# Larger row tiles for a fused residual add and RMS norm: two x slots of 7 rows and a shared residual area in place of three slots of 6 rows

## The chip, the cores and the metric

The kernel runs on one core of a Trainium2 chip. The metric is the device time of one execution in microseconds (us). Nine executions of the kernel before on one chip lie within 1.1 to 1.7 us of each other (the four of the first comparison within 0.7 us), so differences of 1 to 4 us, a tenth of a per cent of the time, can be told apart only with several runs on the same chip.

## The reference

```python
x, residual: float32 [32, 2048, 2048]; gamma: float32 [2048]; eps = 1e-6
z = x + residual
rms = np.sqrt(np.mean(z ** 2, axis=-1, keepdims=True) + eps)
return (z / rms * gamma).astype(np.float32)
```

There are 65,536 rows of 2048 floats (8 KiB each), 512 rows for each of the 128 partitions. Each element is read twice from memory (x and residual) and written once, 1610.6 MB in all.

## The kernel before

A tile has R rows in every partition. Partition p of a tile holds R consecutive rows, so one DMA moves 128 runs, one per partition, of R x 8 KiB. Three slots hold x, and then z and the result in place; one slot holds the residual.

```python
R = 6
NZ = 3
sizes = ([left] if left else []) + [R] * n_full      # 2 rows, then 85 tiles of 6
z_slots = [slots.tile([P, R, D], fp32, name=f"z{k}") for k in range(NZ)]
r_slot = slots.tile([P, R, D], fp32, name="r_slot")
gamma_tile = slots.tile([P, D], fp32, name="gamma_tile")

def compute(i):
    # ... the last tile: pieces of 2 rows, the scale one piece behind ...
    groups = [(a, min(a + 3, sizes[i])) for a in range(0, sizes[i], 3)]
    rms_of = []
    for a, b in groups:
        add(i, a, b)                     # VectorE: z = x + r
        rms_of.append(square(i, a, b))   # ScalarE: sum of squares of each row, then sqrt
    for (a, b), rms in zip(groups, rms_of):
        scale(i, a, b, rms)              # VectorE: 1/rms, then z * rstd * gamma, row by row

load_x(0); load_r(0); load_gamma(); load_x(1); load_r(1)
compute(0)
for i in range(1, n_tiles):
    store(i - 1)
    if i + 1 < n_tiles:
        load_x(i + 1)
    compute(i)
    if i + 1 < n_tiles:
        load_r(i + 1)
store(last)
```

All loads and stores of x, residual and output are issued by SyncE, on one queue; gamma is loaded by ScalarE's queue.

Of the kernel before, what the change touches and what calls it, by code (L numbers as in the profile page):

```python
# [1 line left out]

# [4 lines left out]


@with_exitstack
def kernel(  # L10
    ctx: ExitStack,
    tc: tile.TileContext,
    x: bass.AP,
    residual: bass.AP,
    gamma: bass.AP,
    eps: float,
    out: bass.AP,
):





    nc = tc.nc
    P = nc.NUM_PARTITIONS
    fp32 = mybir.dt.float32
    Act = mybir.ActivationFunctionType
    mult = mybir.AluOpType.mult

    x_f = x.flatten_outer_dims()  # L30
    r_f = residual.flatten_outer_dims()
    o_f = out.flatten_outer_dims()

    n_rows, D = x_f.shape
    R = 6
    NZ = 3
    n_full = n_rows // (P * R)
    left = (n_rows - n_full * P * R) // P
    assert n_full * P * R + left * P == n_rows
    sizes = ([left] if left else []) + [R] * n_full  # L40
    starts = [0]
    for k in sizes:
        starts.append(starts[-1] + P * k)
    n_tiles = len(sizes)
    assert n_tiles >= 4

    def rows(t, i):
        k = sizes[i]
        a = starts[i]
        return t[a : a + P * k, :].rearrange("(p r) m -> p r m", r=k)  # L50

    inv_d = 1.0 / float(D)

    slots = ctx.enter_context(tc.tile_pool(name="slots", bufs=1))
    stats = ctx.enter_context(tc.tile_pool(name="stats", bufs=6))
    psum = ctx.enter_context(tc.tile_pool(name="psum", bufs=1, space=bass.MemoryType.PSUM))

    z_slots = [slots.tile([P, R, D], fp32, name=f"z{k}") for k in range(NZ)]
    r_slot = slots.tile([P, R, D], fp32, name="r_slot")
    gamma_tile = slots.tile([P, D], fp32, name="gamma_tile")  # L60
    eps_tile = slots.tile([P, 1], fp32, name="eps_tile")
    sq_junk = psum.tile([P, D], fp32, name="sq_junk")
    nc.vector.memset(eps_tile, float(eps))  # L63

    last = n_tiles - 1
    piece = 2

    def pieces(i):
        k = sizes[i]
        return [(a, min(a + piece, k)) for a in range(0, k, piece)] if i == last else [(0, k)]  # L70

    def r_of(i):

        return z_slots[NZ - 1] if i == 0 else r_slot

    def load_x(i):
        nc.sync.dma_start(out=z_slots[i % NZ][:, : sizes[i], :], in_=rows(x_f, i))  # L77

    def load_r(i):
        for a, b in pieces(i):  # L80
            nc.sync.dma_start(out=r_of(i)[:, a:b, :], in_=rows(r_f, i)[:, a:b, :])  # L81

    def store(i):
        for a, b in pieces(i):
            nc.sync.dma_start(out=rows(o_f, i)[:, a:b, :], in_=z_slots[i % NZ][:, a:b, :])

    def add(i, a, b):
        z = z_slots[i % NZ]
        nc.vector.tensor_add(out=z[:, a:b, :], in0=z[:, a:b, :], in1=r_of(i)[:, a:b, :])  # L89

    def square(i, a, b):
        n = b - a
        ssq = stats.tile([P, 3], fp32, name="ssq")
        for g in range(n):
            nc.scalar.activation(  # L95
                out=sq_junk,
                in_=z_slots[i % NZ][:, a + g, :],
                func=Act.Square,
                accum_out=ssq[:, g : g + 1],
            )  # L100
        rms = stats.tile([P, 3], fp32, name="rms")
        nc.scalar.activation(  # L102
            out=rms[:, :n], in_=ssq[:, :n], func=Act.Sqrt, bias=eps_tile, scale=inv_d
        )
        return rms

    def scale(i, a, b, rms):
        n = b - a
        rstd = stats.tile([P, 3], fp32, name="rstd")
        nc.vector.reciprocal(out=rstd[:, :n], in_=rms[:, :n])  # L110
        for g in range(n):
            row = z_slots[i % NZ][:, a + g, :]
            nc.vector.scalar_tensor_tensor(  # L113
                out=row,
                in0=row,
                scalar=rstd[:, g : g + 1],
                in1=gamma_tile,
                op0=mult,
                op1=mult,
            )  # L120

    def compute(i):
        if i == last:
            before = None
            for a, b in pieces(i):
                add(i, a, b)
                rms = square(i, a, b)
                if before is not None:
                    scale(i, *before)
                before = (a, b, rms)  # L130
            scale(i, *before)
            return
        groups = [(a, min(a + 3, sizes[i])) for a in range(0, sizes[i], 3)]
        rms_of = []
        for a, b in groups:
            add(i, a, b)
            rms_of.append(square(i, a, b))
        for (a, b), rms in zip(groups, rms_of):
            scale(i, a, b, rms)


    def load_gamma():
        nc.vector.memset(gamma_tile, 0.0)  # L143
        for q in range(4):
            nc.scalar.dma_start(
                out=gamma_tile[32 * q : 32 * q + 1, :], in_=gamma.partition_broadcast(1)
            )
        nc.vector.stream_shuffle(gamma_tile, gamma_tile, [0] * 32)  # L148

    load_x(0)  # L150
    load_r(0)
    load_gamma()
    load_x(1)
    load_r(1)
    compute(0)
    for i in range(1, n_tiles):
        store(i - 1)
        if i + 1 < n_tiles:
            load_x(i + 1)
        compute(i)  # L160
        if i + 1 < n_tiles:
            load_r(i + 1)
    store(last)


# [1 line left out]
_INS = ['x', 'residual', 'gamma', 'eps']  # L167
_OUTS = [((32, 2048, 2048), 'float32')]

_NUMBERS = {'eps': 9.999999974752427e-07}  # L170


# [26 lines left out]
```

## Time and profile before

| | before |
|---|---|
| time, median of 4 runs | 3728.59 us (3728.27 to 3728.93) |
| bytes moved | 1610.6 MB, 432 GB/s over the span |
| DMA engines busy | 100.0% of the span |
| VectorE, ScalarE busy | 62%, 29% |

The lines below are from the page of the kernel before: the span, the busy time of the engines, the DMA rows of the table of 40 slices (busy tenths, then GB/s), and the queue table (packets, MB, share of the 16 DMA engines).

```profile
span 3726.4 us, 2716 instructions
DVE 2312.2 (62%) x860; ACT 1079.1 (29%) x1198; POOL 0.2 (0%) x4
...
DMA  9999999999999999999999999999999999999999
GB/s 421 431 434 433 433 435 431 434 434 433 433 434 432 436 432 432 436 431 434 434 432 434 434 433 435 432 433 436 431 434 434 433 436 433 433 435 432 435 434 398
...
q1 hardware_dynamic: 37728, 1610.63, 100.0%
q14 instruction: 20, 0.16, 0.0%
```

The DMA row has no slice below nine tenths. The queue q1, which carries all loads and stores, fills the 16 engines for the whole span. In this steady part nothing that makes VectorE or ScalarE faster can be expected to help; only fewer bytes, cheaper transfers, or less time in which the DMA stands still. Queue q14 is the fetching of instructions, 20 packets of 8 KiB.

What the DMA queue itself waits for before it can issue (the waits of SyncE's queue; columns: who, for what, us in total, times, longest) shows how far ahead it runs:

```profile
SPq L81 <- DMA r_slot<-in_residual_dram: 1294.7, 84, 16.5
SPq L85 <- DVE z L113: 1192.4, 87, 20.8
SPq L81 <- DVE rstd L110: 1107.2, 84, 13.3
```

L81 is the residual load, L85 the store. SyncE waits most of the time, but it does so with earlier transfers queued, so the waits cost nothing. This has to be checked for each change: a wait of the issuing queue is free only while something else is still in the queue.

One more view is needed, which the page only sums up: the packet records of the trace. Every packet has a start and a duration, and one DMA ends with 16 semaphore packets, one from each engine. From these the following can be read for each engine:

```
packet        most frequent duration (before)
8 KiB run     309 ns
16 KiB run    611 ns
48 KiB run    1815 ns   (24,834 of 32,384)
semaphore     9 ns
time from one semaphore packet to the next on one engine (8 packets of 48 KiB and a semaphore): 14,500 ns
```

The 16 engines do not finish together. In the profiled run of before the median engine's last semaphore packet comes 3718.9 us after the first packet, the slowest engine's at 3723.4 us. The records carry no engine number: "slowest" and "median" are read from the 16 semaphore packets of each DMA, sorted by time.

### The profile page before, as it was taken

How to read it: one execution, taken by the hardware profiler on the slowest of the kernel's cores; microseconds unless marked ns; L12 is line 12 of the kernel's file. 1: busy time of each engine (PE TensorE's matmuls, PEld its weight loads, DVE VectorE, ACT ScalarE, POOL GpSimd, SP SyncE). 2: the span in 40 equal slices, each digit the busy share in tenths (PEclk: the TensorE clock that was granted, in tenths of full speed). 3: DMA queues.
4: the chain of work that ended last, by engine and by line, in shares of the span. 5: the costliest groups of instructions: out<-in, count | busy, mean ns of one | idle time of the engine just before them, and what ended most of it. 6: DMA issues, size and time to landing. Idle time of an engine off the chain costs nothing.

```text
span 3726.4 us, 2716 instructions
## 1 busy us (share of the span) xinstructions
DVE 2312.2 (62%) x860; ACT 1079.1 (29%) x1198; POOL 0.2 (0%) x4
## 2 busy tenths in 40 slices
DVE  5665556666655666665566666556666655566666
ACT  2322222332222233222223332222233222223322
POOL 0000000000000000000000000000000000000000
DMA  9999999999999999999999999999999999999999
GB/s 421 431 434 433 433 435 431 434 434 433 433 434 432 436 432 432 436 431 434 434 432 434 434 433 435 432 433 436 431 434 434 433 436 433 433 435 432 435 434 398
DMA packets 37756, 1610.83 MB, mean 432 GB/s; under 512 B 4196, under 2 KB 4196, under 8 KB 4196
## 3 DMA queue, kind: packets, MB, share of 16 engines
q1 hardware_dynamic: 37728, 1610.63, 100.0%
q14 instruction: 20, 0.16, 0.0%
q10 hardware_dynamic: 8, 0.03, 0.0%
HBM read 1073.77 MB, written 536.87 MB: 432 GB/s over the span
## 4 chain that ended last, share of the span: by engine, by line
DMA 69%; DVE 30%; issue 0%; DVEq 0%; SPq 0%
DMA r_slot<-in_residual_dram 69%; DVE z L89 30%; DVE z L113 0%; DVE rstd L110 0%; DVEq L194 0%; DVEq L89 0%; SPq L77 0%; SPq L81 0%
## 5 line engine op out<-in xcount | busy, mean ns | idle before, releaser
L89 DVE TENSOR_TENSOR z<-z,r_slot 128x6144 f32<-128x6144 f32 (+1 forms) x171 | 1107.6, 6517 | 1380.4 <-DMA r_slot<-in_residual_dram 1380.4
L95 ACT ACTIVATE sq_junk<-z 128x2048 f32<-128x2048 f32 x512 | 963.5, 1882 | 2620.5 <-DVE z L89 2604.1
L113 DVE SCALAR_TENSOR_TENSOR z<-z,rstd,gamma_tile 128x2048 f32<-128x2048 f32 x512 | 1173.8, 2348 | 6.1
L95 ACT ACTIVATION_READ_ACCUMULATOR sq_junk<-z 128x1 f32 x512 | 95.5, 186 | 0.0
L102 ACT ACTIVATE rms<-ssq,eps_tile 128x3 f32<-128x3 f32 (+1 forms) x172 | 51.0, 296 | 5.5
L110 DVE RECIPROCAL rstd<-rms 128x3 f32<-128x3 f32 (+1 forms) x172 | 29.7, 172 | 3.3 <-ACT rms L102 3.2
L89 DVE TENSOR_TENSOR z<-z,z 128x4096 f32<-128x4096 f32 x1 | 4.4, 4426 | 11.4 <-DMA z<-in_residual_dram 11.4
L95 ACT ACT_TABLE_LOAD x1 | 1.3, 1283 | 4.4 <-issue 4.4
L148 DVE STREAM_SHUFFLE gamma_tile<-gamma_tile 128x2048 f32<-128x2048 f32 x1 | 2.5, 2536 | 0.0
L143 DVE MEMSET gamma_tile<- 128x2048 f32 x1 | 1.8, 1765 | 0.4 <-issue 0.4
L102 ACT ACT_TABLE_LOAD x1 | 1.3, 1283 | 0.0
L63 DVE MEMSET eps_tile<- 128x1 f32 x1 | 0.1, 59 | 0.8 <-PEq L180 0.8
L180 POOL MEMSET const-bfloat16-1.0<- 128x1 bf16 x1 | 0.1, 101 | 0.0
L180 POOL MEMSET const-uint8-127<- 128x1 uint8 x1 | 0.1, 101 | 0.0
L180 POOL MEMSET const-float32-0.0<- 128x1 f32 x1 | 0.1, 98 | 0.2 <-issue 0.2
L180 POOL MEMSET const-float32-1.0<- 128x1 f32 x1 | 0.1, 98 | 0.0
L148 DVE LOAD_MASK_SELECT gamma_tile<-gamma_tile x1 | 0.0, 14 | 0.0
## 6 DMA issues: line engine op xcount, KB each, us to landing
z<-in_x_dram SPq DMA_DIRECT2D x85, 6144.0 KB, 44.9
r_slot<-in_residual_dram SPq DMA_DIRECT2D x84, 6144.0 KB, 30.4
out_dram<-z SPq DMA_DIRECT2D x84, 6144.0 KB, 30.8
out_dram<-z SPq DMA_DIRECT2D x4, 2048.0 KB, 15.1
r_slot<-in_residual_dram SPq DMA_DIRECT2D x3, 2048.0 KB, 27.3
z<-in_x_dram SPq DMA_DIRECT2D x1, 2048.0 KB, 7.8
z<-in_residual_dram SPq DMA_DIRECT2D x1, 2048.0 KB, 13.2
gamma_tile<-in_gamma_dram ACTq DMA_DIRECT2D x4, 8.0 KB
```

Source lines behind the costliest of these rows:

```text
L63: nc.vector.memset(eps_tile, float(eps))
L89: nc.vector.tensor_add(out=z[:, a:b, :], in0=z[:, a:b, :], in1=r_of(i)[:, a:b, :])
L95: nc.scalar.activation(out=sq_junk, in_=z_slots[i % NZ][:, a + g, :], func=Act.Square, accum_out=ssq[:, g : g + 1],)
L102: nc.scalar.activation(out=rms[:, :n], in_=ssq[:, :n], func=Act.Sqrt, bias=eps_tile, scale=inv_d)
L110: nc.vector.reciprocal(out=rstd[:, :n], in_=rms[:, :n])
L113: nc.vector.scalar_tensor_tensor(out=row, in0=row, scalar=rstd[:, g : g + 1], in1=gamma_tile, op0=mult, op1=mult,)
L143: nc.vector.memset(gamma_tile, 0.0)
L148: nc.vector.stream_shuffle(gamma_tile, gamma_tile, [0] * 32)
L180: nc = _bacc.Bacc("TRN2", target_bir_lowering=False, num_devices=1)
```

## The change

The intent is to use the on-chip memory for longer runs: 56 KiB in place of 48, so fewer DMAs and fewer packets for the same bytes. Two x slots of 7 rows and a residual area of 11 rows take the place of three x slots and one residual slot of 6 rows. Residual tiles enter the area at row 0 or row 4 in turn, so the next residual tile overlaps the present one only in three rows, and those three rows are added first. Gamma moves to PSUM. 512 = 73 x 7 + 1, so the first tile has 1 row.

```diff
-    R = 6
-    NZ = 3
+    R = 7
+    STEP = 4
...
-    z_slots = [slots.tile([P, R, D], fp32, name=f"z{k}") for k in range(NZ)]
-    r_slot = slots.tile([P, R, D], fp32, name="r_slot")
-    gamma_tile = slots.tile([P, D], fp32, name="gamma_tile")
+    z_slots = [slots.tile([P, R, D], fp32, name=f"z{k}") for k in range(2)]
+    r_area = slots.tile([P, R + STEP, D], fp32, name="r_area")
+    gamma_tile = psum.tile([P, D], fp32, name="gamma_tile")
...
+    def entry(i):
+        if i == 0:
+            return R + STEP - left
+        return 0 if i % 2 else STEP
+
+    tail = [(0, 3), (3, 5), (5, 7)]
+
+    def parts(i):
+        if i == 0:
+            return [(0, left)]
+        return [(STEP, R), (0, STEP)] if i % 2 else [(0, R - STEP), (R - STEP, R)]
...
     load_x(0)
     load_r(0)
     load_gamma()
-    load_x(1)
     load_r(1)
     compute(0)
-    for i in range(1, n_tiles):
+    store(0)
+    load_x(1)
+    load_x(2)
+    compute(1)
+    load_r(2)
+    for i in range(2, n_tiles):
         store(i - 1)
-        if i + 1 < n_tiles:
-            load_x(i + 1)
         compute(i)
         if i + 1 < n_tiles:
             load_r(i + 1)
+            load_x(i + 1)
     store(last)
```

With two slots, x of tile i+1 goes where tile i-1 was, so its load must wait until store(i-1) has landed. Before, it waited for store(i-2), which had landed long ago.

More of the change, by code (lines that the diff above doesn't have):

```diff
@@ L34 @@
     n_rows, D = x_f.shape
-    R = 6
-    NZ = 3
+    R = 7
+    STEP = 4
     n_full = n_rows // (P * R)
     left = (n_rows - n_full * P * R) // P
-    assert n_full * P * R + left * P == n_rows
-    sizes = ([left] if left else []) + [R] * n_full
+    assert n_full * P * R + left * P == n_rows and 0 < left <= STEP
+    sizes = [left] + [R] * n_full
     starts = [0]
@@ L44 @@
     n_tiles = len(sizes)
-    assert n_tiles >= 4
+    last = n_tiles - 1
+    assert n_tiles >= 5
     def rows(t, i):
         k = sizes[i]
-        a = starts[i]
-        return t[a : a + P * k, :].rearrange("(p r) m -> p r m", r=k)
+        return t[starts[i] : starts[i] + P * k, :].rearrange("(p r) m -> p r m", r=k)
     inv_d = 1.0 / float(D)
@@ L63 @@
     nc.vector.memset(eps_tile, float(eps))
-    last = n_tiles - 1
-    piece = 2
-    def pieces(i):
-        k = sizes[i]
-        return [(a, min(a + piece, k)) for a in range(0, k, piece)] if i == last else [(0, k)]
-    def r_of(i):
-        return z_slots[NZ - 1] if i == 0 else r_slot
+    def entry(i):
[7 more added lines that the diff above has]
+        return [(STEP, R), (0, STEP)] if i % 2 else [(0, R - STEP), (R - STEP, R)]
@@ L76, in load_x, with load_r @@
+    def load_r(i):
+        a = entry(i)
+        nc.sync.dma_start(out=r_area[:, a : a + sizes[i], :], in_=rows(r_f, i))
     def load_x(i):
-        nc.sync.dma_start(out=z_slots[i % NZ][:, : sizes[i], :], in_=rows(x_f, i))
-    def load_r(i):
-        for a, b in pieces(i):
-            nc.sync.dma_start(out=r_of(i)[:, a:b, :], in_=rows(r_f, i)[:, a:b, :])
+        for a, b in tail if i == last else [(0, sizes[i])]:
+            nc.sync.dma_start(out=z_slots[i % 2][:, a:b, :], in_=rows(x_f, i)[:, a:b, :])
@@ L83, in store @@
     def store(i):
-        for a, b in pieces(i):
-            nc.sync.dma_start(out=rows(o_f, i)[:, a:b, :], in_=z_slots[i % NZ][:, a:b, :])
+        for a, b in tail if i == last else [(0, sizes[i])]:
+            nc.sync.dma_start(out=rows(o_f, i)[:, a:b, :], in_=z_slots[i % 2][:, a:b, :])
     def add(i, a, b):
-        z = z_slots[i % NZ]
-        nc.vector.tensor_add(out=z[:, a:b, :], in0=z[:, a:b, :], in1=r_of(i)[:, a:b, :])
+        z = z_slots[i % 2][:, a:b, :]
+        o = entry(i)
+        nc.vector.tensor_add(out=z, in0=z, in1=r_area[:, o + a : o + b, :])
@@ L91, in square @@
     def square(i, a, b):
         n = b - a
-        ssq = stats.tile([P, 3], fp32, name="ssq")
+        ssq = stats.tile([P, 4], fp32, name="ssq")
         for g in range(n):
@@ L96, in square @@
                 out=sq_junk,
-                in_=z_slots[i % NZ][:, a + g, :],
+                in_=z_slots[i % 2][:, a + g, :],
                 func=Act.Square,
@@ L100, in square @@
             )
-        rms = stats.tile([P, 3], fp32, name="rms")
+        rms = stats.tile([P, 4], fp32, name="rms")
         nc.scalar.activation(
@@ L108, in scale @@
         n = b - a
-        rstd = stats.tile([P, 3], fp32, name="rstd")
+        rstd = stats.tile([P, 4], fp32, name="rstd")
         nc.vector.reciprocal(out=rstd[:, :n], in_=rms[:, :n])
         for g in range(n):
-            row = z_slots[i % NZ][:, a + g, :]
+            row = z_slots[i % 2][:, a + g, :]
             nc.vector.scalar_tensor_tensor(
@@ L124, in compute @@
             before = None
-            for a, b in pieces(i):
+            for a, b in tail:
                 add(i, a, b)
@@ L132, in compute @@
             return
-        groups = [(a, min(a + 3, sizes[i])) for a in range(0, sizes[i], 3)]
-        rms_of = []
-        for a, b in groups:
+        done = []
+        for a, b in parts(i):
             add(i, a, b)
-            rms_of.append(square(i, a, b))
-        for (a, b), rms in zip(groups, rms_of):
-            scale(i, a, b, rms)
+            done.append((a, b, square(i, a, b)))
+        for d in done:
+            scale(i, *d)
     def load_gamma():
-        nc.vector.memset(gamma_tile, 0.0)
+        row = R + STEP - left - 1
+        stage = r_area[:, row, :]
+        nc.vector.memset(stage, 0.0)
         for q in range(4):
             nc.scalar.dma_start(
-                out=gamma_tile[32 * q : 32 * q + 1, :], in_=gamma.partition_broadcast(1)
+                out=r_area[32 * q : 32 * q + 1, row, :], in_=gamma.partition_broadcast(1)
             )
-        nc.vector.stream_shuffle(gamma_tile, gamma_tile, [0] * 32)
+        nc.vector.stream_shuffle(gamma_tile, stage, [0] * 32)
     load_x(0)
```

## The prediction

> **What bounds the kernel now.** The DMA engines. The profile's table of slices has them at nine tenths or more in all 40 slices, the queue table gives the one load/store queue 100.0% of the 16 engines' span, at 432 GB/s mean (433 to 434 in the middle). VectorE is busy 62%, ScalarE 29%. The Trainium skill, "DMA: Bandwidth & Descriptors", section Bandwidth, gives 435.2 GB/s as the ceiling of the 16 ports; this trace agrees at 434.
>
> **What a packet costs.** The packet records are sharply peaked: 8 KiB in 309 ns, 16 KiB in 611 ns, 48 KiB in 1815 ns (24,834 of 32,384 exactly so). That is a line: 27.2 bytes per ns plus about 9 ns per packet; a semaphore packet is 9 ns more. A 56 KiB packet is then 2116 ns (estimate from this line).
>
> **What the change removes.** Bytes stay at 1610.6 MB. Load/store DMAs fall from 262 to 226, so each engine runs 8 x 36 = 288 packets and 36 semaphore packets fewer: 324 x 9 ns = 2.9 us of about 3720 us per engine. That is on the critical path.
>
> **What it adds.** With two x slots, x(i+1) must wait for store(i-1) to land. In steady state this is hidden: a tile is three transfers of 8 x 2116 ns = 16.9 us, in order store(i-1), residual(i+1), x(i+1). The residual load waits only for tile i's first add (3 rows, 6.55 us), which ends some 10 us before store(i-1) does; x(i+1) can be issued some 15 us before the residual load ends; and a tile's compute (about 33.5 us: adds 15.3, then 7 scales of 2.35 behind squares of 1.88 + 0.19) fits well inside the 50.8 us period. I expect no starvation per tile.
>
> One gap at the start: after x(1) lands, only x(2) and residual(2), 33.9 us, are queued, while store(1) needs 33.5 us of compute, then issue and start (a load's packets begin about 1.6 us after issue, estimated by aligning packet and instruction records). Most engines go idle about 3 us once; those that lag (about 2 us behind by then in the semaphore packets) 1 to 2 us. The laggards set the end: before, most engines finish about 4.5 us ahead of the last. So this costs some 1.5 us. At the end the pieces (3, 2, 2 rows) are ready before the queue reaches them; neutral. Gamma in PSUM and larger adds touch only VectorE, off the path.
>
> **Sum.** 3728.7 - 2.9 + 1.5 = 3727.3 us. Range 3723 to 3732. Faster by over 2%: 1%; within 2%: 98%; slower by over 2%: 1%.
>
> **What would show the steps right or wrong.**
> - Packets 37,756 before, near 32,600 after; 56 KiB packets at 2116 ns.
> - DMA share full in every slice; mean 432 GB/s again.
> - DMA queue's waits: residual load released by the first add, x load by the store's landing, both while earlier transfers run. In the timeline store(1) is issued near 80 us, about when residual(2) ends, and DMA dips just after.
> - VectorE near 2305 us; the gamma-in-PSUM scale near 2.35 us.
>
> **What would make it wrong.** The residual load waiting for both adds or a later VectorE instruction; a start latency of stores of many us, so that the queue runs dry per tile (each us per tile is 73 us, 2%); the 56 KiB address pitch suiting memory worse or better than 48 KiB; lagging engines lagging further, which the mean share would hide.

## The result

| | before | changed |
|---|---|---|
| time, median of 4 runs | 3728.59 us (3728.27 to 3728.93) | 3730.61 us (3729.46 to 3732.38) |
| ratio | | 1.0006, 95% interval 0.9988 to 1.0023 |
| span of the profiled run | 3726.4 us | 3728.7 us |

A ratio is the mean time of one kernel's runs over that of the other's of the same rounds, so it is not quite the ratio of the medians. By the ratio alone the two are the same. Repeated twice more with 5 runs each, on chips 12 and 13, the changed kernel took 3731.40 (3730.44 to 3733.40) beside 3728.79 (3728.07 to 3729.14), and 3730.68 (3729.40 to 3731.89) beside 3728.79 (3728.05 to 3729.37). In each of the three comparisons its fastest run is above the slowest of before: it is about 2 us slower, where the prediction expected 1.4 us faster.

The page of the changed kernel, the same lines:

```profile
span 3728.7 us, 2557 instructions
DVE 2301.9 (62%) x812; ACT 1071.7 (29%) x1174; POOL 0.2 (0%) x4
...
DMA  9999999999999999999999999999999999999999
GB/s 408 423 433 433 434 433 434 433 434 435 433 433 433 433 433 434 434 434 434 434 433 435 434 434 433 433 433 433 433 434 434 434 435 434 434 434 434 433 433 403
...
q1 hardware_dynamic: 32544, 1610.63, 99.9%
q14 instruction: 20, 0.16, 0.0%
```

Packets are down as planned. The middle of the run is as fast as before or a little faster; the first two slices, 408 and 423 against 421 and 431, are slower. The waits of the DMA queue (L82 is the residual load, L90 the store, L86 the x load):

```profile
SPq L82 <- DVE z L95: 1682.0, 72, 24.6
SPq L90 <- DVE z L119: 1195.0, 75, 32.0
SPq L86 <- DMA out_dram<-z: 717.9, 72, 11.5
```

The third line is the new dependence: 72 times the x load waited for a store to land. It looks like the cost of the change at first sight. The periods say otherwise: from 300 to 3600 us a DMA of 7 rows takes the median engine 16,920 ns, or 2417.1 ns per row, against 14,512 ns, or 2418.7 ns per row, before. Over 512 x 3 = 1536 rows that is 2.4 us less. So the wait is hidden, as predicted. On the slowest engine the same stretch shows no saving, 2421.0 to 2422.0 ns per row in three profiled runs of the changed kernel against 2420.8 before; the records further below tell why.

The slow first slices are seen in the timeline of SyncE's queue (start us, us, engine, line, instruction, what it moves):

```profile
20.55 0.35 SPq L90 DMA_DIRECT2D out_dram<-z  x1
20.95 10.05 SPq L86 DMA_DIRECT2D z<-in_x_dram  x2
54.10 0.33 SPq L82 DMA_DIRECT2D r_area<-in_residual_dram  x1
80.54 0.34 SPq L90 DMA_DIRECT2D out_dram<-z  x1
88.03 0.33 SPq L82 DMA_DIRECT2D r_area<-in_residual_dram  x1
```

x(2) and residual(2) are the only work behind x(1). Store(1) is issued at 80.54 us, when residual(2) has already ended on nearly all engines. The same stretches by windows (from:to in us, length, busy time and count of VectorE, ScalarE and GpSimd, PE clock, DMA share, GB/s), first of before and then of the changed kernel:

```profile
70.00:78.00 8.00, 2.35 (x2) 0.00 (x0) 0.00 (x0) 1.00 0.99 430
78.00:82.00 4.00, 2.87 (x1) 0.00 (x0) 0.00 (x0) 1.00 1.08 467
82.00:90.00 8.00, 8.00 (x2) 4.22 (x5) 0.00 (x0) 1.00 0.96 418
```

```profile
70.00:78.00 8.00, 6.79 (x4) 1.11 (x3) 0.00 (x0) 1.00 0.96 416
78.00:82.00 4.00, 3.07 (x3) 0.00 (x0) 0.00 (x0) 1.00 0.57 244
82.00:90.00 8.00, 8.00 (x2) 1.97 (x2) 0.00 (x0) 1.00 0.98 423
```

From 78 to 82 us the DMA moves 244 GB/s in place of 467: the queue has run dry once. (Short windows hold few packets of 2 us each, so a share can come out above 1.) In the records the idle time there is 2.6 us, averaged over the engines.

There is a second dry stretch, which was not predicted, near 3706 us: 3.2 us of mean idle time. At the end of the run VectorE does all three adds of the last tile before the first scale, although the code writes a scale between the second and the third. The scheduler had reordered them.

```profile
3684.31 15.23 DVE L95 TENSOR_TENSOR z<-z,r_area 128x6144 f32<-128x6144 f32 x3 [8.18 <-DMA z<-in_x_dram]
...
3701.67 11.36 DVE L119 SCALAR_TENSOR_TENSOR z<-z,rstd,gamma_tile 128x2048 f32<-128x2048 f32 x5
```

The kernel before has an idle stretch in its tail as well, of 1.2 us. The windows of the tail, of before and then of the changed kernel (mind the different ends):

```profile
3700.00:3710.00 10.00, 9.93 (x7) 4.74 (x8) 0.00 (x0) 1.00 0.84 360
```

```profile
3702.00:3710.00 8.00, 8.00 (x4) 3.75 (x5) 0.00 (x0) 1.00 0.51 222
```

So 2.6 us of mean idle time at the start and 3.2 - 1.2 = 2.0 us more in the tail stand against 2.4 us saved. The simple sum, 2.6 + 2.0 - 2.4 = 2.2 us, is just what the profiled runs differ by. The experiments show that this sum is nevertheless the wrong explanation: it fits by chance.

### The profile page after: what moved, and what is told of

It reads as the page before. It is cut to its first block, busy times and chain, and to the rows that moved or that the text cites. A ratio compares the mean times of both kernels' runs of the same rounds, so it can differ in the third digit from the quotient of the medians.

```text
span 3728.7 us, 2557 instructions
## 1 busy us (share of the span) xinstructions
DVE 2301.9 (62%) x812; ACT 1071.7 (29%) x1174; POOL 0.2 (0%) x4
## 2 busy tenths in 40 slices
DMA packets 32572, 1610.82 MB, mean 432 GB/s; under 512 B 3620, under 2 KB 3620, under 8 KB 3620
## 4 chain that ended last, share of the span: by engine, by line
DMA 67%; DVE 24%; ACT 8%; issue 0%; DVEq 0%; ACTq 0%; SPq 0%
DMA z<-in_x_dram 33%; DMA out_dram<-z 33%; DVE z L95 15%; DVE z L119 9%; ACT sq_junk L101 8%; DMA r_area<-in_residual_dram 1%; DMA r_area<-in_gamma_dram 0%; ACT rms L108 0%; DVE rstd L116 0%; DVE gamma_tile L155 0%; DVEq L204 0%; DVE r_area L150 0%; ACTq L152 0%; DVEq L95 0%; SPq L90 0%
## 5 line engine op out<-in xcount | busy, mean ns | idle before, releaser
L95 DVE TENSOR_TENSOR z<-z,r_area 128x6144 f32<-128x6144 f32 (+3 forms) x148 | 1109.0, 7535 | 1293.7 <-DMA z<-in_x_dram 1287.1
L116 DVE RECIPROCAL rstd<-rms 128x3 f32<-128x3 f32 (+3 forms) x148 | 25.6, 173 | 111.1 <-ACT rms L108 111.1
L108 ACT ACTIVATE rms<-ssq,eps_tile 128x3 f32<-128x3 f32 (+3 forms) x148 | 43.9, 297 | 4.8
## 6 DMA issues: line engine op xcount, KB each, us to landing
r_area<-in_residual_dram SPq DMA_DIRECT2D x73, 7168.0 KB, 27.2
```

What stands on the lines that cost most here:

```text
L95: nc.vector.tensor_add(out=z, in0=z, in1=r_area[:, o + a : o + b, :])
L108: nc.scalar.activation(out=rms[:, :n], in_=ssq[:, :n], func=Act.Sqrt, bias=eps_tile, scale=inv_d)
L116: nc.vector.reciprocal(out=rstd[:, :n], in_=rms[:, :n])
```

## The experiments

The theories:

- **A.** The slowest of the 16 DMA engines sets the end. The loss is the dry stretch near 80 us, as far as that engine feels it, and slow packets after it; the dry stretch in the tail costs nothing, because the slowest engine is behind and never runs dry there.
- **B.** Every microsecond of mean idle time counts, at the start and in the tail.
- **C.** The loss is in the steady state: two slots or the 56 KiB runs.

Eleven kernels ran, one of them (the changed kernel unaltered) twice, so twelve runs. All gave correct results.

| run | time, median us (range) | before on the same chip |
|---|---|---|
| after_again (changed kernel) | 3731.40 (3730.44 to 3733.40) | 3728.79 |
| start_fix | 3732.22 (3731.09 to 3733.05) | 3728.79 |
| tail_fix | 3731.01 (3730.47 to 3733.82) | 3728.79 |
| both_fix | 3732.37 (3731.72 to 3733.89) | 3728.79 |
| store_split | 3727.62 (3725.74 to 3729.27) | 3729.00 |
| split3 | 3763.72 (3763.66 to 3763.88) | 3729.00 |
| pad_act | 3731.55 (3731.00 to 3731.94) | 3729.00 |
| pad_pool | 3728.89 (3728.75 to 3729.21) | 3729.00 |
| gamma_first | 3726.27 (3725.83 to 3727.12) | 3728.79 |
| after_same_chip (changed kernel) | 3730.68 (3729.40 to 3731.89) | 3728.79 |
| split2 | 3746.42 (3746.34 to 3746.60) | 3728.79 |
| gamma_tail | 3726.92 (3726.18 to 3727.36) | 3728.35 |

Every ratio to before has a 95% interval of about plus or minus 0.13 to 0.16%, some 5 us; differences of less are argued from the ranges of the runs on one chip and from the records, not from these intervals.

### after_again and after_same_chip: the anchor

> The changed kernel unaltered, as the anchor of this chip. Expected 3729.5 to 3732.5 us, about 2 us above before. If it lies within 0.5 us of before here, the first difference was chance and nothing is left to explain.

> The unaltered changed kernel once more, as the anchor for gamma_first on one chip: 3729.5 to 3733.5 us, as on the two chips so far.

Both as expected. The difference of 2 us is no chance of one chip.

### tail_fix: the tail's dry stretch

```diff
+                if a == tail[-1][0]:
+                    with tc.issue_after(scaled):      # scaled: the last scale of the first piece
+                        add(i, a, b)
```

> The changed kernel with the last piece's add held behind the first piece's scales on VectorE, as the code's order meant it, so that the first piece's store is ready about 4 us earlier and the dry stretch near 3706 us (3.2 us mean) shrinks. Theory A (the slowest DMA engine, which never runs dry there, sets the end): most engines finish 2 to 4 us earlier, the time moves by less than 0.7 us. Theory B (mean idle counts): 2 to 3 us less. Theory C: no change either; start_fix tells A from C.

The windows of the tail, of after_again and then of tail_fix, on the same chip:

```profile
3702.00:3710.00 8.00, 7.21 (x5) 4.91 (x8) 0.00 (x0) 1.00 0.38 165
3710.00:3720.00 10.00, 8.91 (x5) 0.00 (x0) 0.00 (x0) 1.00 0.98 416
3720.00:3725.00 5.00, 0.00 (x0) 0.00 (x0) 0.00 (x0) 1.00 0.99 423
3725.00:3730.00 5.00, 0.00 (x0) 0.00 (x0) 0.00 (x0) 1.00 0.50 213
```

```profile
3702.00:3710.00 8.00, 7.96 (x5) 0.78 (x2) 0.00 (x0) 1.00 0.81 346
3710.00:3720.00 10.00, 8.71 (x5) 3.65 (x5) 0.00 (x0) 1.00 0.87 369
3720.00:3725.00 5.00, 0.00 (x0) 0.00 (x0) 0.00 (x0) 1.00 0.89 380
3725.00:3730.00 5.00, 0.00 (x0) 0.00 (x0) 0.00 (x0) 1.00 0.06 26
```

The edit did its work: from 3702 to 3710 us the DMA share rises from 0.38 to 0.81, and after 3725 us nearly all engines are done (share 0.06 in place of 0.50). In the records the median engine ends at 3723.1 us after the first packet in place of 3726.1. The time did not move: 3731.01 against 3731.40 us, with the slowest engine ending at 3726.2 and 3726.9 us. Theory B falls here: an end 3 us earlier on most of the engines was worth nothing that can be told from the scatter of the runs.

### start_fix and both_fix: a fix that moved the dry stretch

```diff
-    sizes = [left] + [R] * n_full
+    sizes = [left + 1, R - 1] + [R] * (n_full - 1)      # 2, 6, 7, 7, ...
...
     load_r(1)
+    load_x(1)
     compute(0)
     store(0)
-    load_x(1)
     load_x(2)
```

Not shown: the parts of tile 1 end at its 6 rows, and the load of residual(2) is held behind that of x(2).

> The changed kernel with tiles 0 and 1 of 2 and 6 rows in place of 1 and 7, and x(1) issued before store(0), so that 38 us of transfers stand behind x(1) while tile 1 is computed. Theory A (the slowest DMA engine sets the end; the dry queue of 2.6 us mean near 80 us and the slow restart of all engines in step after it, about 2 us each, are the loss): no idle near 80 us, no slow packets near 100 and 132 us, and 2 to 3 us less than the changed kernel. Theory B (every mean idle microsecond counts): 2.6 us less. Theory C (the loss is in the steady state: two slots, 56 KiB runs): no change within 0.7 us.

> Both edits together. Theory A: as start_fix, 2 to 3 us less than the changed kernel, at or up to 1.5 us under before. Theory B: 5 to 6 us less than the changed kernel, 3 us under before. Theory C: no change.

Neither gained. The expectation "no idle" was mistaken, and the timeline of start_fix shows why:

```profile
29.42 0.35 SPq L92 DMA_DIRECT2D out_dram<-z  x1
...
44.92 13.03 DVE L97 TENSOR_TENSOR z<-z,r_area 128x4096 f32<-128x4096 f32 x2 [15.53 <-DMA z<-in_x_dram]
...
49.71 0.33 SPq L87 DMA_DIRECT2D z<-in_x_dram  x1
```

Store(0) was now the last thing in the queue, behind x(1), and x(2) goes into the slot that store(0) empties. So x(2) could be issued only when the slowest engine had finished store(0), at 49.71 us, and the queue was dry for 3.8 us of mean idle time: the dry stretch had moved from 80 to 50 us. As the cost stayed the same too (3732.22 against 3731.40 us, the ranges overlap), this miss fits theory A, but it does not decide between A and C.

### store_split: the dry stretch at the start, taken away

```diff
     def store(i):
-        for a, b in tail if i == last else [(0, sizes[i])]:
+        cut = tail if i == last else parts(1) if i == 1 else [(0, sizes[i])]
+        for a, b in cut:
```

> The changed kernel with store(1) alone cut into its two parts of 3 and 4 rows, so that the first part can go out about 70 us after the start, while residual(2) still runs. Theory A (dry queue near 80 us, the restart of all engines in step, and the slowest engine setting the end): no dip of the DMA near 80 us, the slowest engine's records lose the 1.6 us stop, and the time falls by 1.5 to 4 us against the unaltered changed kernel (3731.4 us), to 3727.5 to 3730. Theory C (steady state): no change within 0.7 us.

3727.62 us, within what theory A expected, though on another chip than after_again (before took 3729.00 us on this chip and 3728.79 on that one, so the chips differ little). One store, cut in two, out of 226 DMAs brought 3 to 4 us; theory C falls. The spread was wide. In the profiled run, which is the slowest of the five (3729.27 us), gamma landed at 19.7 us in place of 15.8, store(0) was late in consequence, and the queue ran dry near 25 us.

### gamma_first: both dry spots at the start taken away

```diff
         for q in range(4):
-            nc.scalar.dma_start(
+            nc.sync.dma_start(
                 out=r_area[32 * q : 32 * q + 1, row, :], in_=gamma.partition_broadcast(1)
             )
```

On top of store_split, the gamma loads now stand in the same queue behind residual(0) and ahead of residual(1).

> The changed kernel with store(1) cut in two as in store_split, and the four loads of gamma issued on the same queue as x and residual, ahead of residual(1), so that gamma lands by about 10 us and store(0) is ready before the queue empties near 24 us in every run (in the profiled run of store_split gamma landed at 19.7 us and the queue ran dry there). Theory A: no dry stretch before the tail; about 1 us less than store_split on average and less spread, 3725.5 to 3728, and 3 to 5 us under the unaltered changed kernel on the same chip. Theory C: as the unaltered changed kernel.

3726.27 us, 4.4 us under the unaltered changed kernel on the same chip (3730.68), with no overlap of the ranges. It holds two edits, and the move of gamma alone was not run; store_split, without it, stood 3 to 4 us below the changed kernel on other chips. The timeline of SyncE's queue and the windows of the profiled run:

```profile
3.05 1.17 SPq L153 DMA_DIRECT2D r_area<-in_gamma_dram  x4
4.26 0.36 SPq L82 DMA_DIRECT2D r_area<-in_residual_dram  x1
19.09 0.37 SPq L91 DMA_DIRECT2D out_dram<-z  x1
...
69.98 11.19 SPq L91 DMA_DIRECT2D out_dram<-z  x2
```

```profile
70.00:78.00 8.00, 6.50 (x4) 1.40 (x3) 0.00 (x0) 1.00 1.06 459
78.00:82.00 4.00, 3.06 (x3) 0.00 (x0) 0.00 (x0) 1.00 0.88 377
82.00:90.00 8.00, 8.00 (x2) 1.67 (x1) 0.00 (x0) 1.00 1.02 441
```

The first half of store(1) is issued at 69.98 us, while residual(2) still runs, and in the records no engine is idle before the tail. This version is also below the kernel before, by 2.5 us (ratio 0.9994, interval 0.998 to 1.0007; the ranges 3725.83 to 3727.12 and 3728.05 to 3729.37 do not meet).

The records tell how a dry stretch that stops the slowest engine for 1.6 us grows into a larger loss. The table gives, for the slowest engine of the profiled runs, the time of its semaphore packets beyond a nominal sum (27.2046 bytes per ns, from the difference of the spacings of 16,909 and 14,500 ns for DMAs of 7 and 6 rows, and the 46 ns that are left for each DMA), at the end of the first DMA after each of several times of the run:

```
                 nominal   60 us  130 us  220 us  660 us  1800 us  3600 us   end    end, us after the first packet
before           3712.3     4.3     4.3     5.0     5.8      7.4     11.0   11.1    3723.4
changed          3710.6     4.2     7.0     7.5    10.3     11.6     14.9   15.0    3725.6
after_same_chip  3710.6     3.5     6.0     6.6     9.3     11.0     15.2   15.3    3725.9
gamma_first      3710.7     4.5     4.5     5.4     6.5      7.2     10.1   10.3    3721.0
pad_act          3712.3     4.0     4.5     4.5     5.8      8.4     14.0   14.1    3726.3
```

- Between 60 and 130 us the slowest engine of the changed kernel loses 2.8 us: 1.6 us of it is the stop (its records of store(1) lie 18.5 us behind those of residual(2), where 16.9 is the transfer), the rest is slow packets after the restart.
- Up to there it had been 2.3 us behind the median engine. The stop lets it catch up, to 0.2 us. That is no gain, because from 220 to 660 us it falls back again by 2.3 us, losing 2.8 us to slow packets where before loses 0.8.
- At 660 us the six profiled runs with a dry stretch at 50 or 80 us (changed, after_again, after_same_chip, tail_fix, start_fix, both_fix) stand at 8.9 to 11.3 us, and the five without one before the tail (before, gamma_first, gamma_tail, pad_act, pad_pool) at 5.4 to 6.6. Store_split, dry for 0.9 us near 25 us, stands at 7.1.
- From 660 us on, all of them but pad_act lose another 3.8 to 6.7 us, in no order that follows the start (gamma_first 3.8, changed 4.7, before 5.2, gamma_tail 5.5, after_same_chip 6.0). So some 2 of the 5 us between the profiled runs of gamma_first and after_same_chip come after 660 us and are not shown to be an effect of the start.

The slow packets near the start hit all 16 engines together (in the changed kernel packets of 2.8 to 4.1 us in place of 2.1 near 23 us, and of 2.5 to 3.6 us near 96 and 131 us; in store_split a packet of 2.9 to 3.6 us near 77 us, at the end of residual(2)), at times when their packets start nearly together: within 0.2 to 0.5 us of each other in these cases, but for one engine near 23 us. Before and gamma_first have one such case each, near 40 and near 22 us. Why these packets are slow is not settled by these runs, nor that starting together is the reason. That the lag is rebuilt is seen in the records of each run that had a dry stretch near the start (changed, after_again, after_same_chip, start_fix, tail_fix, both_fix, store_split); it was not tested by itself.

### gamma_tail: the tail once more

The edit of tail_fix on top of gamma_first.

> gamma_first and the tail's order of tail_fix together. In gamma_first the slowest engine is only 2.7 us behind when the tail comes, so there, unlike in the changed kernel, it does run dry: its record of the first tail piece ends 9.6 us after the store before, where 7.25 us is the transfer. Theory A (the slowest engine's own idle time counts, nobody else's): the same tail edit that gave nothing on the changed kernel now gives 1.5 to 2.3 us, 3723.5 to 3725 us, against 3726.3 for gamma_first; 4 to 5 us under before. If the tail edit gives nothing here either, the slowest engine is not what ends the kernel. If it had been worth its mean idle time, it would have given 3 us in both.

3726.92 us, no gain over gamma_first (3726.27 us, on another chip; against before 0.9996 and 0.9994). The expectation was built on a wrong reading. The four gamma loads in the same queue add four semaphore packets, on a single engine, and these had shifted my grouping of the records by four. Read rightly, the slowest engine of gamma_first is 4.9 us behind in the tail, not 2.7, and its first tail piece ends 7.27 us after the store before, so it does not run dry there either. With that, theory A expects no gain, and there is none; but this is a reading after the fact. The clean test of the tail is tail_fix.

### pad_act and pad_pool: what makes an engine slow

In the records of before, each of the 20 instruction fetches (8 KiB) hits one DMA engine: it takes 309 ns in itself, between two packets of the load queue, and mostly also slows a packet by 300 to 500 ns. For most fetches (16 of 20 in before) the engine that is hit can be followed, packet by packet, to the semaphore packet of its DMA, and so its place among the 16 is known.

```diff
+        for _ in range(8):      # pad_act; pad_pool has nc.gpsimd.tensor_copy(out=pad_out, in_=rms_of[-1][:, :1])
+            nc.scalar.activation(out=pad_out, in_=rms_of[-1][:, :1], func=Act.Square)
```

> The kernel before with 8 tiny ScalarE instructions added behind each tile's squares, 680 in all, about 0.2 us each, off the path; they add 5 instruction fetches of 8 KiB on the DMA. Theory A (the end is set by the one DMA engine that carries most of the instruction fetches, each about 0.7 us there): 2.5 to 4 us more, if ScalarE's fetches are that engine's. Theory B (mean of the engines): 5 x 0.7 / 16 = 0.2 us more.

> The same 680 tiny instructions on GpSimd, whose instructions are otherwise only a handful, so that the 5 fetches may fall on another DMA engine, which is about 4.5 us ahead of the last. Theory A: under 1 us more if it is another engine; as pad_act if it is the same one, which the trace shows. Theory B: 0.2 us more.

The queue table's line of instruction fetches, of pad_act and then of pad_pool:

```profile
q14 instruction: 26, 0.20, 0.0%
```

```profile
q14 instruction: 27, 0.22, 0.0%
```

Nearly the same number of fetches was added, 6 and 7. Pad_act took 3731.55 us, 2.5 us more than before; pad_pool 3728.89, no more than before. ScalarE was busy for 1079 us and had ample room for 138 us of padding, so this is not its time. The slowest DMA engine of pad_act ended 3.0 us later beyond its nominal (table above). At 3600 us, before the tail, its slowest engine stands at 14.0 us beyond the nominal and its median engine at 4.1, against 11.0 and 5.1 in before: the delay is not one of all engines. The records show where the fetches went. In pad_act one series of them, about every 240 us, hits an engine whose lag behind the median grows from 0 us at 90 us to 9.9 us at 3472 us, and which is the last of the 16 from 1289 us on. In pad_pool six of the seven that were added, about every 610 us, hit an engine that is 0.8 us behind at 278 us and 4.0 us at 3371 us, and never the last. Theory A holds: the fetches of ScalarE's instructions fall on the engine that sets the end, those of GpSimd on one that has time to spare. The mean over the engines cannot tell these two kernels apart.

### split2 and split3: what a packet costs

On the kernel before, each transfer of 6 rows cut into two of 3 rows or three of 2:

```diff
-        return [(a, min(a + piece, k)) for a in range(0, k, piece)] if i == last else [(0, k)]
+        step = piece if i == last else 2          # split2: 3
+        return [(a, min(a + step, k)) for a in range(0, k, step)]
```

and the same cut in the x load.

> The kernel before with each transfer of 6 rows cut into two of 3 rows: runs of 24 KiB, 253 DMAs more. By the spacing of the semaphore packets (46 ns a DMA) 11.6 us more, and with the slow packets that came with each added DMA in split3 (55 ns a DMA in its steady part) 14 us; by the durations alone (81 ns a DMA) 20.5 us. A dry stretch in the tail, 6 us in split3, may come on top and is to be read from the trace.

> The kernel before with each transfer of 6 rows cut into three of 2 rows: runs of 16 KiB in place of 48, 506 DMAs and so 4,048 data packets more on each engine. If a record costs 9 ns more of wall time, as the prediction had it from the durations alone: 506 x 81 ns = 41 us more. If consecutive packets overlap by 3 to 4 ns, so that a DMA of 8 packets and a semaphore has 46 ns over its bytes, as the spacing of the semaphore packets in both traces says: 23 us more. If run length itself mattered to memory: far more than either.

The queue table's line of split3 shows the packets, almost three times those of before:

```profile
q1 hardware_dynamic: 110592, 1610.66, 100.2%
```

| | DMAs more | time more | steady part: ns per row, median engine | steady part x 1536 rows, more than before | per added DMA |
|---|---|---|---|---|---|
| before | | | 2418.7 | | |
| split2 | 253 | 17.6 us | 2427.4 | 13.3 us | 53 ns |
| split3 | 506 | 34.7 us | 2436.4 | 27.2 us | 54 ns |

Neither the 81 ns that the durations gave nor the 46 ns of the undisturbed spacing is right: the steady part costs 53 to 54 ns per DMA, in proportion to their number. (A DMA of 16 KiB runs takes 4862 ns, 44 ns over its bytes at the same rate; the rest is slow packets.) The remainder of the added time, 4 and 8 us, falls outside the steady part; the records show the engines dry in the tail for 5.2 and 9.2 us there (before 1.2), and this was not followed further. For the changed kernel 36 DMAs fewer at 54 ns are 1.9 us, and its own steady rows give 2.4 us.

## Why the prediction was right or wrong

The measured 3730.61 us lies within the range of 3723 to 3732, and "within 2%" was the right class. The centre, 1.4 us faster, had the wrong sign. The range was 9 us wide and held both signs, so that hitting it says little: both terms of the sum erred in the same direction, the saving by 1.2 us and the cost by 2.4 us, as the points below tell.

- **What bounds the kernel: right.** The DMA share is full in both pages and VectorE's busy time (2301.9 us; 2305 predicted) is off the path. The Trainium skill ("DMA: Bandwidth & Descriptors", section Bandwidth) gives 435.2 GB/s for the 16 ports, and the middle of both runs moves 433 to 434 on average, just under it.
- **The 56 KiB packet: right.** 2116 ns was predicted and is the most frequent duration (20,849 of 27,776). There were 32,572 packets, near 32,600 as predicted.
- **"324 x 9 ns = 2.9 us": somewhat too large.** Durations were summed, but in the records a packet starts 3 to 4 ns before the one ahead of it ends. The spacing of the semaphore packets gives 46 ns for a DMA of 8 packets and a semaphore, not 81, and split2 and split3 measure 54 with the slow packets in. The saving was 2.4 us on the median engine in the steady part; by the nominal sum it is 36 x 46 ns = 1.7 us, and on the slowest engine it is lost among its slow packets.
- **"No starvation per tile": right.** The x load waited 72 times for a store to land, and the DMA rate of the middle did not suffer.
- **"One gap at the start": right in place and size, wrong in its consequences.** 3 us were predicted for most engines and 1 to 2 for the laggards; 2.6 us on average and 1.6 us on the slowest were measured. The step that failed is "so this costs some 1.5 us". Slow packets at the restart and the slowest engine's falling back behind the others came on top. In total the slowest engine ended 15.0 us beyond its nominal in place of 11.1, so the term measured 3.9 us in the profiled runs (4.5 us by 660 us, 0.6 us less after it); taking the dry spots away brought 4.4 us. The prediction itself had named "lagging engines lagging further" among the things that would make it wrong. With the nominal 1.7 us less (36 x 46 ns), 3.9 - 1.7 = 2.2 us is the difference of the profiled runs (3730.5 and 3728.3 us).
- **"At the end the pieces are ready before the queue reaches them": wrong, without effect.** The scheduler's order on VectorE made the first piece late, and most engines ran dry for 3.2 us on average. It is neutral all the same, because the slowest engine did not; tail_fix showed this. Before had 1.2 us of idle time there too.
- **"The laggards set the end": right**, and the most useful sentence of the prediction; tail_fix and pad_act against pad_pool bear it out.

Still open: why packets of all engines are slow together, why a lag that was lost is rebuilt, why the runs lose between 3.8 and 6.7 us after 660 us, and why the changed kernel spreads over 2.5 to 3 us from run to run where before spreads over 0.7 to 1.7.

## What to carry to other kernels

In a kernel whose DMA is always busy, larger transfers buy only a fixed cost per DMA, here about 54 ns, so count the DMAs before spending memory on them. Fewer slots take away the queue's reserve, and the place to check is not the steady state but the first tiles, where a store may have to wait for a whole tile's compute with too little queued behind it; cutting that one store in two brought more than the whole change of the tile size. Look at the slowest of the 16 engines, by its semaphore packets, and not at the mean share: idle time on the other 15 cost nothing in the tail here, and instruction fetches can decide which is the slowest.

## What the Trainium skill lacked or had wrong

- "DMA: Bandwidth & Descriptors", section Anatomy of one DMA: it fits about 2.0 us fixed for each DMA, for GpSimd-issued DMAs, and lacks the price of one DMA more in a queue that is always full. Here 253 and 506 DMAs more, issued by SyncE, cost 53 and 54 ns each in the steady part. The page's section Rules for kernel authors says that the fixed cost overlaps with compute when a DMA is issued early, but gives no figure for DMAs that overlap each other.
- The same page, section Why small descriptors are slow: about 3 cycles of fixed cost per packet, and combining descriptors is worth it only at 256 B or less. The runs do not contradict it, though a record of the profile need not be a packet of the page: going from 48 to 56 KiB saves 2.4 us of 3729 on the median engine. The section lacks the cost in time; the spacing gives 46 ns for 9 records, about 5 ns each (an estimate).
- The same page, section Queues, rings and completion order: it states that an engine goes round between the queues it has work for and that row 14 is internal to the runtime. It lacks that instruction fetches there (20 packets of 8 KiB in before, each mostly 309 ns and 300 to 500 ns of slowing) come again and again on the same engine and can set the end: 6 more for ScalarE cost 2.5 us, 7 more for GpSimd nothing. "Runtime: NRT & Kernel Launch", section Instruction fetch mechanics, lacks it as well.
- The same page, section Why a DMA increments its semaphore by 16 and not by 1: the engines finish independently. No page says how far apart they get; here the slowest was 4.5 us behind the median at the end of before and 5 to 6 us in the middle of the changed kernel's tail.
- The same page, section Bandwidth, says in a note that about 358 GB/s bind for transfers between HBM and SBUF, which does not hold for one core alone (the page's own rule above the note ties that figure to both cores of the domain streaming); with this one core active the kernel moved 432 over its span. The page's own measurement of 425 and this one agree.
- No page was found that describes slow packets of all 16 engines at once (2.5 to 4.1 us in place of 2.1).
